# A planned decoder layer: buffers placed by the planner, loads reckoned by run length, v's norm two steps later, and two moves to ScalarE

## The chip, the cores and the metric

The kernel runs on one core of a Trainium2 chip. The time is the device time of one execution in microseconds (us); it was taken three times for the kernel before. Five engines work side by side, each with its own queue of instructions in order: TensorE (PE; its weight loads are shown as PEld), VectorE (DVE), ScalarE (ACT), GpSimd (POOL) and SyncE (SP), which issues most of the transfers between HBM and the on-chip memory. Results of PE land in PSUM, all else lies in SBUF.

## The reference

One layer of a decoder trunk, for a prompt of 1024 tokens and 8 single-token samples, D = 1024, all in float32:

```
xn = rmsnorm(h, pre_g);  u, v, z_a, x_b, z_b, g_a, g_b = split(xn @ w_in)      # 1024 x 7168
vn = layernorm(gelu(v));  s = tril(w_s[g]) @ vn (within chunks of 128 tokens) + b_s[g]
y_a = gelu(u) * s * silu(z_a)
q = trailing mean of x_b over 2/4/8/16 tokens - x_b;  y_b = (q @ w_pool) * scale * silu(z_b)
m = sigmoid(g_a) * (y_a @ w_pa) + sigmoid(g_b) * (y_b @ w_pb)
h = h + rmsnorm(m @ w_out, post_g)
e = p @ w_ple;  h = h + rmsnorm(sigmoid(rmsnorm(h, ple_in_g) @ w_pg) * e, ple_out_g)
```

Further outputs are the normed v of the last chunk and of the samples, and the last rows of x_b.

## The kernel before

**Precision and products.** Every float32 operand is cut into two parts, high and low (`split`, line 341: ACT writes the high part, DVE the rest), and a product is three products on PE (high x high, high x low, low x high; `product`, line 568). The large products are done by a Strassen scheme (`strassen`, line 616): seven products P1 to P7 in place of eight, over quarters of x (B11, B21, B22) and sums of quarters (T1 to T4), and over quarters or sums of the weight. One such product of a quarter is a step: `prepare` cuts its weight part, `run` issues its 12 matmuls of 512 columns (two of 260 where the 8 samples ride along), `evacuate` takes the PSUM result. The first evacuation, of P1, opens a buffer u: ACT copies 512 columns into it and, where the samples ride along, POOL zeroes the last 8 (line 632). Later parts are added to u on DVE.

**Order of the stages.** Opening (`begin`, line 1584): the embedding e = p @ w_ple, the norm and turning of x, the first steps of v. Then v (4 pairs of feature blocks), g_a, u with z_a, x_b with z_b and the pooling, g_b, the products with w_pa and w_pb (all with features on the partitions), and then, with tokens on the partitions (`Tokens`, line 540; PSUM tile `acct`), m @ w_out (`outsteps`) and the gate product with w_pg (`gatesteps`). At the very start PE transposes the identity ten times into a PSUM bank named warm (line 1607).

**v's norm.** v is written to HBM in 32 x 32 blocks (`V.done`, line 870; runs of 128 bytes), read back a chunk of 128 tokens at a time (`v_fetch`), turned back block by block on DVE, summed and squared on ACT (`ln_stats`), scaled (`ln_apply`), cut into vh and vl (`v_split`) and multiplied with the chunk's w_s on PE (`spatial`, PSUM tile `mix`). These calls are hung on the steps of g_a and of the first u and z_a (line 1259): for the n-th chunk at s = 3 + 4n the fetch at step s - 2, the stats and the norm at s, the cut at s + 1, the products at s + 4.

**The gate's norm.** After m @ w_out a tile of h (128 tokens) is scaled by the post norm, h's old value is added by a transfer, its squares are summed on ACT into the buffer hn, DVE scales h into hn (`gate_norm`, line 1382), and PE transposes hn (tile `pht`).

**The planner** (line 55). The program's calls are not issued at once: each is recorded as an Op with an estimated duration. A call of PE advances a clock; `at` of an Op is that clock when it was recorded. `wanted` (line 172) works back from PE's `at` to the latest moment `late` at which each Op must start. `order` (line 195) then plays the engines forward: an Op may start when its inputs are there, its engine is free, and not before min(late - lead, at) + slip; among those that could start, the one with the earliest `late` is taken. So the order on PE may differ from the program's. `slip` is how far PE is behind: start - at of the last PE Op (line 268). A transfer is reckoned at 0.36 MB per us whatever its shape, plus a fixed landing time.

**Slots.** All larger buffers come from a pool of 46 equal slots (line 321). Before, the pool handed out its buffers in turn: `row` in `order` lists freed slots by the order in which their last user was issued, a new buffer takes the front of it, and it waits for that slot's last user. A transfer wants 3 slots to spare.

Of the kernel before, what the change touches and what calls it, by code (L numbers as in the profile page):

```python
# [45 lines left out]

class Taker:
# [7 lines left out]
class Planner:  # L55
# [8 lines left out]
    LOAD, LEAD, PATIENCE, RATE, SPARE = 14.0, 14.0, 60.0, 0.36, 3  # L64
    SPARED = 1.0

    def __init__(self, nc, slots, queues):
        self.nc, self.slots, self.queues = nc, slots, queues
        self.ops, self.seen, self.users, self.tags = [], {}, {}, {}
        self.fixed, self.open, self.clock = True, None, 0.0  # L70
        for e in self.ENGINES:
            setattr(self, e, Taker(self, e))

    def tile(self, ap, tag):

        self.tags[ap.tensor.name] = tag
        return ap

    def space(self, ap):
# [18 lines left out]
        return ap.tensor.name, first, first + parts, tuple(pieces)  # L98

# [38 lines left out]
    def take(self, engine, method, args, kwargs):  # L138
# [56 lines left out]
    def order(self):  # L195
# [10 lines left out]
        row, slip, table, pipe, done = [((0, -1), 0.0)] * self.slots, 0.0, 1, 0.0, 0  # L206
        calls = []
# [4 lines left out]
        def soonest(o):  # L212
# [18 lines left out]
        while done < len(self.ops):  # L231
# [23 lines left out]
            del row[: len(o.fresh)]  # L255
# [11 lines left out]
            elif e == "tensor" and not o.fixed:  # L267
                slip = max(0.0, o.start - o.at)
# [9 lines left out]
            for name in o.names:  # L278
                if name in left:
                    left[name] -= 1  # L280
                    last[name] = max(last[name][0], key), max(last[name][1], end)
                    if not left[name]:
                        row.append((last[name][0], last[name][1] + 0.3))
            row.sort(key=lambda r: r[0])
        return [(e, call) for _, _, e, call in sorted(calls, key=lambda c: c[:2])]

    def play(self, tc):
        with tc.manual_schedule():
            for e, (method, args, kwargs) in self.order():
                getattr(getattr(self.nc, e), method)(*args, **kwargs)  # L290
# [6 lines left out]
def hybrid_step(  # L297
# [9 lines left out]
    spool = ctx.enter_context(tc.tile_pool(name="slots", bufs=SLOTS))  # L307
# [13 lines left out]
    def slot(name, shape=(P, T), dt=F32):  # L321
        n_name[0] += 1
        return plan.tile(spool.tile(list(shape), dt, tag="slot", name=f"{name}_{n_name[0]}", bufs=SLOTS,
                                    padded_shape=None), "slot")
# [39 lines left out]
    for j in range(POOL_BUF):  # L364
        nc.gpsimd.memset(rc[:, j : j + 1], 1.0 / (j + 1))
    nc = plan
# [3 lines left out]

    def rstd(parts, n=P):

        t, r = sm("ms"), sm("rstd")
        nc.vector.tensor_scalar(out=t[:n], in0=parts[0][:n], scalar1=EPS,
                                scalar2=parts[1][:n] if len(parts) == 2 else 0.0, op0=ALU.add, op1=ALU.add)
        nc.gpsimd.tensor_tensor(out=r[:n], in0=t[:n], in1=mhalf[:n], op=ALU.pow)
        return r

    def root(part, n=P):

        t, r = sm("ms"), sm("rstd")
        nc.vector.tensor_scalar(out=t[:n], in0=part[:n], scalar1=EPS, scalar2=None, op0=ALU.add)
# [233 lines left out]
    def strassen(weights, operand, user, form=Features, order=None):  # L616
# [183 lines left out]
    def norm_root(t):  # L800
        xt, n = (xe, NS) if t == S else (xts[t], P)
        roots[t] = root(square_sum(xt[:n], n, scratch=slot("squares", (P, D))), n)
# [6 lines left out]
    nc.scalar.activation(out=warm, in_=mhalf, func=AF.Gelu_apprx_tanh)  # L809
    vecs = slot("vecs", (P, P))  # L810
# [449 lines left out]
    for n, t in enumerate([NB - 1, *range(NB - 1)]):  # L1260
        s = 3 + 4 * n
# [4 lines left out]
        at(flow[s + 4], lambda t=t: spatial(t))  # L1266
# [82 lines left out]
    class Out(User):  # L1349
# [9 lines left out]
        def direct(self, m, j, ps):  # L1359
            t = self.tile(m)  # L1360
            parts[t].append(square_sum(ps))
            nc.scalar.activation(out=h_of[t][:, half(j)], in_=ps, func=AF.Copy)

        def summed(self, m, j, ps, u, free=None):
# [3 lines left out]
            parts[t].append(square_sum(o))  # L1368
# [13 lines left out]
    def gate_norm(t):  # L1382
# [5 lines left out]
        nc.vector.tensor_scalar_mul(hn[:r], h[:r], rs[:r])  # L1388
# [20 lines left out]
    def out_sample():  # L1409
        start(S, "hs")  # L1410
        for j, o in enumerate(sample_product(samples["m"], woop)):
            parts[S].append(square_sum(o[:NS], NS))
# [9 lines left out]
    def gated(t, c, src):  # L1422
# [4 lines left out]
        parts[t].append(square_sum(g, r))  # L1427
        if len(parts[t]) > 2:
            a, b = parts[t][:2]
            both = sm("both")  # L1430
            nc.vector.tensor_scalar(out=both[:r], in0=a[:r], scalar1=b[:r], scalar2=None, op0=ALU.add)
            parts[t][:2] = [both]
# [21 lines left out]
    class Embed(User):  # L1454
        def loads(self):
# [31 lines left out]
    gatesteps = [strassen(Turned(i, "h"), wgop, Embed(i), Tokens, LAST if i == NPAIR - 1 else None)  # L1487
# [15 lines left out]
    at(outsteps[3][4], lambda: gain_row("out", ple_out_g[0]))  # L1503
# [17 lines left out]
    def p_load(h):  # L1521

        praw.append(slot("p", (P, 4, PLE)))
        src = p_prompt[h * HALF : (h + 1) * HALF].rearrange("(p t) c -> p t c", t=4)
        for q in range(2):
            dma(praw[h][:, 2 * q : 2 * q + 2], src[:, 2 * q : 2 * q + 2])
# [57 lines left out]
    def begin():  # L1584
# [22 lines left out]
        for t in range(10):  # L1607
            nc.tensor.transpose(ps[:, t % 4 * P : (t % 4 + 1) * P], ident, ident)
# [6 lines left out]
        embed_out(0, 0)  # L1615
# [87 lines left out]
```

## Time and profile before

| | |
|---|---|
| median of 3 runs | 1004.33 us (1003.48 to 1004.35) |
| the profiled execution, its own time | 1005.86 us |
| its span, first to last instruction | 1004.2 us |
| mean granted clock of PE | 0.993 |
| moved by DMA | 169.04 MB, 168 GB/s over the span |

The busy times in a row of a view are sums over an engine's instructions. The windows of the trace cut the span into stretches and give each engine's busy time in it, then PE's granted clock as a share of full speed, the share of time that the 16 DMA engines were busy, and the GB/s they moved. The waits give, for each engine and tile, the instruction that it waited for: total, times, longest. A row of the timeline gives the start, the duration, the engine and the operation (written tile <- read tiles), and in square brackets how long the engine had been idle before it and what ended that.

### The profile page before, as it was taken

Reading aid. Unit: us, or ns where it says so; the run is one execution under the profiler, and the core shown is the slowest. Engines: PE = TensorE matmul, PEld = TensorE weight load, DVE = VectorE, ACT = ScalarE, POOL = GpSimd, SP = SyncE. Lnnn points to the kernel's source line nnn. Section 1 sums busy time; section 2 is a strip of 40 time slices with the busy share of each in tenths; the row PEclk is TensorE's granted clock in tenths of the full one; section 3 lists DMA queues with packets and bytes.
Section 4 is the critical chain, followed back from the end, with each engine's and each line's share of the span. In section 5 each row is a group of like instructions: output and inputs, shape, how many; then the busy total and the mean of one; then the engine's idle time right before and its main releaser. Section 6 shows DMA issues by size and latency. Waiting matters only on the chain. (4 is left out here: it accounts for less than half of the span.)

```text
span 1004.2 us, 16017 instructions
## 1 busy us (share of the span) xinstructions
PE 984.5 (98%) x6122; PEld 883.1 (88%) x6122; DVE 805.0 (80%) x1239; ACT 487.5 (49%) x845; POOL 81.8 (8%) x162
## 2 busy tenths in 40 slices
PE   8999999999999999999999999999999999998996
PEld 6899988999999999999999999999999988887885
DVE  5698458887788898887776987697799898779796
ACT  7764345666434334232433333552353365678563
POOL 1230000000000000000010100000000002312121
PEclk9999999899999999999999999999999999999998
DMA  9364644333365676441304075973754543397437
GB/s 352 130 148 85 148 105 170 105 127 106 126 221 199 231 273 202 166 170 53 123 15 156 28 257 208 314 279 125 246 218 150 181 153 84 87 304 262 128 78 218
DMA packets 120033, 169.04 MB, mean 168 GB/s; under 512 B 40830, under 2 KB 79790, under 8 KB 119949
## 3 DMA queue, kind: packets, MB, share of 16 engines
q1 hardware_dynamic: 117589, 160.11, 47.0%
q0 software_dynamic: 2048, 7.37, 4.3%
q8 instruction: 48, 0.79, 0.3%
q10 hardware_dynamic: 320, 0.54, 0.2%
q14 instruction: 28, 0.23, 0.1%
HBM read 116.69 MB, written 51.77 MB: 168 GB/s over the span
## 5 line engine op out<-in xcount | busy, mean ns | idle before, releaser
L290 DVE TENSOR_TENSOR u<-acc,u 128x520 f32<-128x520 f32 (+1 forms) x90 | 62.4, 694 | 35.1 <-PE acc L290 31.7
L290 POOL TENSOR_TENSOR rstd<-ms,mhalf 128x1 f32<-128x1 f32 (+1 forms) x45 | 41.0, 913 | 229.7 <-DVE ms L290 214.6
L290 POOL MEMSET u<- 128x8 f32 x35 | 3.6, 104 | 553.4 <-PE acc L290 302.5
L290 ACT ACTIVATE u<-acc 128x512 f32<-128x512 f32 x39 | 23.2, 594 | 37.0 <-PE acc L290 36.4
L290 ACT ACTIVATE paw<-pas 128x512 fp32r<-128x512 f32 x16 | 10.0, 628 | 31.2 <-DVE pas L290 25.9
L290 DVE TENSOR_TENSOR big<-big 128x1024 f32<-128x1024 f32 (+4 forms) x20 | 24.5, 1263 | 0.0
L290 DVE TENSOR_TENSOR xb<-acc,u 128x520 f32<-128x520 f32 (+1 forms) x12 | 8.3, 693 | 19.1 <-PE acc L290 19.1
L290 ACT ACTIVATE zbw<-zbs 128x512 fp32r<-128x512 f32 x16 | 9.9, 628 | 27.8 <-DVE zbs L290 24.5
L290 ACT ACTIVATE pbw<-pbs 128x512 fp32r<-128x512 f32 x16 | 10.0, 629 | 27.2 <-DVE pbs L290 24.0
L290 ACT ACTIVATE big<-pht,gvec 128x128 f32<-128x128 f32 x64 | 17.9, 396 | 7.0 <-PE pht L290 7.0
L290 PE MATMUL accm<-qh,wpoolw 128*128 128x260 f32 (+1 forms) x96 | 20.9, 319 | 0.0
L290 ACT ACTIVATE big<-mix 128x256 f32<-128x256 f32 x32 | 12.0, 381 | 16.9 <-PE mix L290 16.1
L290 DVE TENSOR_TENSOR acc<-acc,u 128x512 f32<-128x512 f32 (+1 forms) x16 | 11.2, 697 | 8.7 <-PE acc L290 8.7
L290 PE MATMUL mix<-wst,vh 128*128 128x256 f32 x64 | 16.6, 335 | 1.4 <-ACT vh L290 0.8
L290 ACT ACTIVATE gbw<-gbs 128x512 fp32r<-128x512 f32 x16 | 10.0, 626 | 15.1 <-DVE gbs L290 12.6
L290 DVE SCALAR_TENSOR_TENSOR zb<-accm,gvec,zb 128x512 f32<-128x512 f32 (+1 forms) x16 | 12.0, 751 | 6.5 <-PE accm L290 6.4
L290 PEld LDWEIGHTS accm<-qh,wpoolw 128*128 128x128 f32 x96 | 15.6, 188 | 1.9
L290 ACT ACTIVATE xbw<-xbs 128x512 fp32r<-128x512 f32 x16 | 9.8, 625 | 15.0 <-DVE xbs L290 12.8
L290 ACT ACTIVATE gb<-gb 128x1032 f32<-128x1032 f32 (+1 forms) x8 | 6.8, 854 | 18.2 <-DVE gb L290 18.2
L290 PE MATMUL mix<-wst,vl 128*128 128x128 f32 x64 | 14.7, 230 | 0.9 <-DVE vl L290 0.9
L290 ACT ACTIVATE uw<-us 128x512 fp32r<-128x512 f32 x16 | 9.9, 626 | 11.5 <-DVE us L290 6.2
L290 DVE TENSOR_TENSOR gaw<-gas,gaw 128x512 fp32r<-128x512 f32 x16 | 11.0, 686 | 5.7 <-ACT gaw L290 5.6
(691 smaller groups left out, 3614.0 us busy)
## 6 DMA issues: line engine op xcount, KB each, us to landing
ga<-ga SPq DMA_DIRECT2D x16, 516.0 KB
gb<-gb SPq DMA_DIRECT2D x16, 516.0 KB
ya<-za SPq DMA_DIRECT2D x8, 516.0 KB
yb<-zb SPq DMA_DIRECT2D x8, 516.0 KB
x<-in_x_prompt_dram SPq DMA_DIRECT2D x8, 512.0 KB
vraw<-in_w_in_dram SPq DMA_DIRECT2D x8, 512.0 KB
e<-e SPq DMA_DIRECT2D x8, 512.0 KB
vturned<-v SPq DMA_DIRECT2D x32, 128.0 KB
```

Source lines behind the costliest of these rows:

```text
L290: getattr(getattr(self.nc, e), method)(*args, **kwargs)
```

## The change

- Loads: a transfer's size is weighed by its shortest contiguous run (`run`): (1 + 0.2 / run in KB), at a rate of 0.42 in place of 0.36 MB per us; one that accumulates counts twice and lands after 3.5 in place of 4.5.
- Slots: each slot has its own buffer. The planner picks the slot when it places an Op: of those already free at that moment in its reckoning, the one freed last (for Ops of the fixed opening the one freed first). An Op waits for as many free slots as it needs. Buffers are made when the plan is played (`View`, `slot`, `real`).
- slip is PE's start less the work that PE has done, not less the Op's own place in the program.
- v's norm: s = 5 + 4n, and the products at s + 5.
- ACT zeroes the end of u (from a constant), after its copy; ACT scales h into hn.
- The opening: nine matmuls of 512 columns with a zeroed tile `heat` (DVE sets it) in place of ten transposes; the first cut of e on DVE; w_ple's first half in two transfers; three short vector loads from ACT's queue to SP's, and w_ple's second half ahead of them.
- Sums of squares of a tile are added as they come (`gather`); the loads for the gate's tiles (`ge_start`) and the gain row for the output are hung on steps later than before (the gain row on the gate's second step in place of the fifth of the last product with w_out).

The core of the diff:

```
@@ Planner @@
-    LOAD, LEAD, PATIENCE, RATE, SPARE = 14.0, 14.0, 60.0, 0.36, 3
+    LOAD, LEAD, PATIENCE, RATE, SPARE = 14.0, 14.0, 60.0, 0.42, 3
...
+    def run(ap):
+        n = 1
+        for s, m in reversed(list(ap.ap)[0 if "DRAM" in str(ap.space) else 1 :]):
+            if m == 1:
+                continue
+            if s != n:
+                break
+            n *= m
+        return min(n * 4e-3, 4.0)
...
-            op.busy, op.moved = 1.0 if engine == "gpsimd" else 0.45, writes[0].size() * 4e-6
-            op.lands = 4.5 if kwargs.get("accum_op") is not None else 2.0
+            run = min(self.run(a) for a in (writes[0], reads[0]))
+            op.busy, op.moved = 1.0 if engine == "gpsimd" else 0.45, writes[0].size() * 4e-6 * (1 + 0.2 / run)
+            op.lands = 2.0
+            if kwargs.get("accum_op") is not None:
+                op.moved, op.lands = 2 * op.moved, 3.5
...
-                t = max(t, *(end for _, end in row[: len(o.fresh)]), *(key[1] for key, _ in row[:need] if key[0]))
+                t = max(t, row[len(o.fresh) - 1][0])
...
-            del row[: len(o.fresh)]
+            could = [r for r in row if r[0] <= now + 1e-9]
+            for name in sorted(o.fresh):
+                r = could.pop(0 if o.fixed else -1)
+                row.remove(r)
+                self.place[name] = r[1]
...
-                slip = max(0.0, o.start - o.at)
+                slip = max(0.0, o.start - worked)
+                worked += o.busy
...
-                        row.append((last[name][0], last[name][1] + 0.3))
-            row.sort(key=lambda r: r[0])
+                        row.append((max(last[name][1] + 0.3, key[1] if key[0] else 0.0), self.place[name]))
+            row.sort()
@@ hybrid_step @@
+    none = cpool.tile([P, NS], F32, tag="none", name="none")
+    nc.gpsimd.memset(none, 0.0)
...
+    def gather(parts, part, n=P):
+        if parts:
+            so_far = sm("sofar")
+            nc.vector.tensor_scalar(out=so_far[:n], in0=parts[-1][:n],
+                                    scalar1=EPS if len(parts) == 1 else parts[0][:n], scalar2=None, op0=ALU.add)
+            parts[:] = [so_far]
+        parts.append(part)
...
+                nc.scalar.activation(out=at["u"][:, :HALF], in_=ps, func=AF.Copy)
                 if form.tail:
-                    nc.gpsimd.memset(at["u"][:, HALF:], 0.0)
-                nc.scalar.activation(out=at["u"][:, :HALF], in_=ps, func=AF.Copy)
+                    nc.scalar.activation(out=at["u"][:, HALF:], in_=none, func=AF.Copy)
...
+    heat = slot("heat", (P, HALF), F32R)
+    nc.vector.memset(f32(heat), 0.0)
...
-        s = 3 + 4 * n
+        s = 5 + 4 * n
...
-        at(flow[s + 4], lambda t=t: spatial(t))
+        at(flow[s + 5], lambda t=t: spatial(t))
...
-        nc.vector.tensor_scalar_mul(hn[:r], h[:r], rs[:r])
+        nc.scalar.activation(out=hn[:r], in_=h[:r], func=AF.Copy, scale=rs[:r])
...
-    at(outsteps[3][4], lambda: gain_row("out", ple_out_g[0]))
+    at(gatesteps[0][1], lambda: gain_row("out", ple_out_g[0]))
+    for i, e in enumerate(embeds):
+        at(gatesteps[i - 1][4] if i else outsteps[3][6], e.begin)
...
-        we.fetch(0, nc.scalar)
+        raw = we.raw[0, 0] = slot("weraw", (P, 2, HALF))
+        for k in range(2):
+            dma(raw[:, k], w_ple[k * P : (k + 1) * P, :HALF], nc.scalar)
         for t in range(4):
             x_load(t)
+        we.fetch(1)
         for i, v in enumerate((pre_g, pool_scale, ple_in_g)):
-            dma(vecs[i * NB : (i + 1) * NB, :], v[0].rearrange("(k p) -> k p", p=P), nc.scalar)
-        we.fetch(1)
+            dma(vecs[i * NB : (i + 1) * NB, :], v[0].rearrange("(k p) -> k p", p=P))
...
-        for t in range(10):
-            nc.tensor.transpose(ps[:, t % 4 * P : (t % 4 + 1) * P], ident, ident)
+        for t in range(9):
+            plan.apart()
+            nc.tensor.matmul(ps, heat[:, :P], heat, start=True, stop=True)
...
-        embed_out(0, 0)
+        embed_out(0, 0, True)
```

More of the change, by code (lines that the diff above doesn't have):

```diff
@@ L205, in order @@
         rings["scalar"] = rings["sync"]
-        row, slip, table, pipe, done = [((0, -1), 0.0)] * self.slots, 0.0, 1, 0.0, 0
-        calls = []
+        row, slip, table, pipe, done = [(0.0, i) for i in range(self.slots)], 0.0, 1, 0.0, 0
+        calls, worked = [], 0.0
         for o in self.ops:
@@ L369, in hybrid_step @@
     big = cpool.tile([P, NB, T], F32, tag="big", name="big")
+    def gather(parts, part, n=P):
[5 more added lines that the diff above has]
+        parts.append(part)
     def rstd(parts, n=P):
         t, r = sm("ms"), sm("rstd")
[L374 to L382, printed above, removed]
+        nc.vector.tensor_scalar(out=t[:n], in0=parts[-1][:n], scalar1=EPS if len(parts) == 1 else parts[0][:n],
+                                scalar2=None, op0=ALU.add)
         nc.gpsimd.tensor_tensor(out=r[:n], in0=t[:n], in1=mhalf[:n], op=ALU.pow)
@@ L801, in norm_root @@
         xt, n = (xe, NS) if t == S else (xts[t], P)
-        roots[t] = root(square_sum(xt[:n], n, scratch=slot("squares", (P, D))), n)
+        roots[t] = rstd([square_sum(xt[:n], n, scratch=slot("squares", (P, D)))], n)
     def norm_scale(t):
@@ L1426, in gated @@
         mul(g, e_of[t][:r, c], g)
[L1427 to L1432, printed above, removed]
+        gather(parts[t], square_sum(g, r), r)
         if t >= NB - 2:
@@ L1454, in hybrid_step, with begin @@
     class Embed(User):
-        def loads(self):
+        def begin(self):
             for m in range(2):
```

61 lines of the change are left out of this document (51 added, 10 removed).

## The prediction

> **What bounds the kernel now.** I read the busy times on the page first, then the windows of 25 us, the waits of PE, short windows where PE stood idle, and the timeline around those places.
>
> ```profile
> PE 984.5 (98%) x6122; PEld 883.1 (88%) x6122; DVE 805.0 (80%) x1239; ACT 487.5 (49%) x845; POOL 81.8 (8%) x162
> ```
> ```profile
> 0.00:25.00 25.00, 21.13 (x100) 17.11 (x100) 12.65 (x24) 17.76 (x29) 4.34 (x27) 1.00 0.99 353
> ...
> 125.00:150.00 25.00, 23.23 (x148) 20.36 (x147) 12.29 (x23) 11.56 (x20) 1.47 (x5) 1.00 0.46 106
> 150.00:175.00 25.00, 23.27 (x164) 21.20 (x162) 22.13 (x40) 13.42 (x23) 1.91 (x3) 1.00 0.48 170
> 175.00:200.00 25.00, 24.51 (x148) 22.97 (x149) 21.05 (x40) 15.45 (x28) 1.54 (x2) 0.87 0.32 106
> ...
> 500.00:525.00 25.00, 25.00 (x167) 22.92 (x166) 18.54 (x29) 6.05 (x11) 3.35 (x6) 1.00 0.11 34
> ...
> 900.00:925.00 25.00, 22.19 (x104) 17.52 (x103) 23.08 (x31) 22.43 (x46) 5.72 (x6) 1.00 0.94 322
> ...
> 975.00:1000.00 25.00, 20.20 (x100) 16.79 (x98) 20.69 (x37) 11.03 (x27) 5.74 (x7) 0.95 0.85 224
> ```
> The columns are the stretch, its length, the busy time of PE, PEld, DVE, ACT and POOL, the granted clock, the DMA share and GB/s. PE is the bound: 984.5 of 1004.2 us. A middle window such as 500 to 525 us is full, so no work taken from another engine gains there; it can only lose. The 19.7 us of idle PE lie in few places: 25 - 21.13 = 3.87 us in the opening, 1.77 + 1.73 + 0.49 = 3.99 us between 125 and 200 (where v is normalised), 2.81 us between 900 and 925 (the start of the gate product), and the rest, some 9 us, is the end after the last matmul. One loss is not idle time: the clock is 0.87 between 175 and 200. So what the change can gain is the opening, v's norm with its clock, and the gate's start.
>
> ```profile
> PE acct L290 <- DVE ms L290: 1.6, 1, 1.6
> PE acc L290 <- DVE ms L290: 1.5, 1, 1.5
> PE acct L290 <- DVE hw L290: 1.2, 1, 1.2
> PE mix L290 <- DVE vl L290: 0.9, 1, 0.9
> PE mix L290 <- ACT vh L290: 0.8, 1, 0.8
> PE mix L290 <- DVE big L290: 0.5, 1, 0.5
> ```
> Each of these is one event, so the schedule that the planner writes is nearly right everywhere and wrong at about five points.
>
> **v's norm, two steps later.** The planner's moved calls (v_fetch, ln_stats, ln_apply, v_split) start at flow[5 + 4n] instead of flow[3 + 4n]; the mix products of the chunk come at +5 instead of +4, so three steps later in all. What failed before:
>
> ```profile
> 147.81 1.21 DVE L290 TENSOR_TENSOR sv<-sv,lng 8x1024 f32<-8x1024 f32 x1
> 148.95 0.68 DVE L290 TENSOR_TENSOR ga<-acc,u 128x520 f32<-128x520 f32 x1
> 149.68 0.51 PE L290 MATMUL acc<-xB22h,gaw 128*128 128x260 f32 x2 [1.48 <-DVE ms L290]
> 165.75 1.25 DVE L290 STREAM_TRANSPOSE big<-vblocks 128x1024 f32<-128x1024 f32 x1 [1.74 <-DMA vblocks<-vturned]
> 172.69 0.39 PE L290 MATMUL mix<-wst,vh 128*128 128x256 f32 x1 [0.83 <-ACT vh L290]
> 173.95 0.33 PE L290 MATMUL mix<-wst,vl 128*128 128x128 f32 x1 [0.87 <-DVE vl L290]
> ```
> At 149.68 PE waits 1.48 us; the evacuation that frees its PSUM region (ga, 148.95 to 149.63) stood behind a 1.21 us norm step in DVE's strict queue. At 172.69 and 173.95 it waits for vh and vl; DVE had itself stood 1.74 us for the block from HBM. After that the clock falls:
>
> ```profile
> 174.50:176.00 1.50, 0.98 (x8) 0.83 (x6) 1.50 (x6) 0.83 (x3) 0.00 (x0) 0.63 0.00 0
> 176.00:178.00 2.00, 2.00 (x11) 2.00 (x10) 1.97 (x6) 1.96 (x5) 0.00 (x0) 0.50 0.00 0
> 178.00:180.00 2.00, 2.00 (x11) 2.00 (x11) 2.00 (x5) 2.00 (x4) 0.55 (x1) 0.50 0.00 0
> 180.00:182.00 2.00, 2.00 (x12) 2.00 (x12) 1.14 (x2) 1.44 (x2) 0.00 (x0) 0.57 0.63 262
> ```
> The clock's loss is length times (1 - clock): 1.5 x 0.37 + 2 x 0.5 + 2 x 0.5 + 2 x 0.43 = 3.4 us. With the waits of 1.48, 0.83, 0.87 and 0.52 this place costs 7.1 us, nearly half of it by the clock. Each chunk moves its fetch on SP, its transpose, norm and cut on DVE, two sums and a cut on ACT and a root on POOL, past the weight loads and cuts of two steps; nothing is added to them. A step is 12 products of 512 columns, 2.8 us (12 x 0.23, the spacing in the opening below). Between fetch and mix there is now one step more, 2.8 us, above the 2.2 us that vh, vl and the next mix were late, and the first fetch comes two steps (5.6 us) after it did, when v's last turned blocks are out. The new reckoning of loads helps the same place: v's turned writes go in runs of 128 bytes, which the planner now counts 1 + 0.2/0.128 = 2.6 times as long as before per byte. What is late next is DVE, at 21 to 22 us of 25 from 150 to 200, with SP behind it (a store of a normed tile waits in SP's queue for DVE, and block fetches behind the store); the moved work is carried into 200 to 260. I take 6.0 us of the 7.1 as gained; bounds 7.1 and 0.
>
> **The opening.** Ten transposes of the identity become nine products of a zeroed 128x512 tile; the first cut of e goes to DVE; w_ple comes in two pieces; the three vector loads go from ACT's queue to SP's.
>
> ```profile
> 1.93 2.40 PE L290 MATMUL warm<-ident 128*128 128x128 f32 x10 [1.93 <-POOL ident masks.py:199]
> 6.84 0.60 ACT L290 ACTIVATE ph<-pp 128x512 fp32r<-128x512 f32 x1 [4.54 <-DMA p<-in_p_prompt_dram]
> 8.60 0.63 PE L290 MATMUL e<-wehi,pl 128*128 128x512 f32 x1
> 9.03 0.63 PE L290 MATMUL e<-wehi,ph 128*128 128x512 f32 x1
> 11.58 0.39 PE L290 MATMUL e<-wehi,pl 128*128 128x512 f32 x1
> 11.80 0.39 PE L290 MATMUL e<-wehi,ph 128*128 128x512 f32 x1
> 12.92 1.03 ACT L290 ACTIVATE e<-e 128x1024 f32<-128x1024 f32 x1 [1.89 <-PE e L290]
> 25.96 0.48 PE L290 MATMUL acc<-xB11h,vw 128*128 128x512 f32 x1
> ```
> ```profile
> 8.01:11.34 3.33, 3.33 (x8) 2.67 (x9) 2.53 (x6) 3.02 (x6) 0.55 (x1) 1.00 1.02 411
> ```
> The products of e start 0.43 us apart (8.60, 9.03) until 11, then 0.23 (11.58, 11.80), although the clock column of the window says 1.00: the spacing shows a cold array that the column doesn't. Eight products in 3.33 us would take 8 x 0.23 = 1.8 warm, so 1.5 us are lost. Nine zero products take 9 x 0.43 = 3.9 us; with a memset of DVE ahead, behind which all of PE's queue stands (no row; between nothing and the 0.7 us of a 128x512 step of DVE), they run from about 1.5 to 5.5 us. p's transposes of the first half then wait till 5.5 us, covered: their cut stood until 6.84 us on ACT anyway. That cut can now begin at about 6.1 us, since ACT no longer issues vector loads; worth 0.7 us if w_ple has landed. Against it stands DMA: its share is 0.99 over the first 25 us, and x and w_in still come at the same rate, so part of what PE gains it waits out later. The vector loads lengthen SP's queue ahead of w_in's first tiles, which nobody needs before 25.96 us. Moving e's 1.03 us from ACT to DVE (about 1.4 us there, two pieces of 0.7) relieves ACT, busy 17.76 us of 25 against DVE's 12.65. Bounds: 0 (all is given back to DMA) and 2.2 (1.5 + 0.7). I take 1.3, a little over the middle, since the rows show both an array that is cold and DMA engines that are full.
>
> The Trainium skill's page "TensorE: Matmul & The Clock Gate", Part 4, says that transposes do not count as busy for the gate; the trace agrees (PE transposed from 1.93 us on and was still cold at 9.03). But Part 1 of that page speaks against the change: one idle window of about 3.4 us brings the gate down again, and between the zero products and e there are only transposes. By it the opening could keep its cold products; this is the second rival.
>
> **The gate's start.** The scaling of h goes to ACT, 8 tiles and the sample.
>
> ```profile
> L290 ACT ACTIVATE hn<-h x8: 1042/1060/1078, 845.6 to 923.1; 128x1024 f32<-128x1024 f32 x8
> L290 DVE TENSOR_SCALAR hn<-h,rstd x8: 731/746/753, 849.5 to 927.7; 128x1024 f32<-128x1024 f32 x8
> 914.59 2.35 DVE L290 TENSOR_TENSOR wgT4l<-wgT,wgT4h 128x1024 fp32r<-128x1024 f32 x2
> 916.86 0.68 DVE L290 TENSOR_TENSOR hw<-big,hw 128x512 fp32r<-128x512 f32 x1
> 917.60 0.73 PE L290 MATMUL acct<-wgT4h,hw 128*128 128x512 f32 x2 [1.24 <-DVE hw L290]
> ```
> PE waits at 917.60 for a cut that DVE did after two cuts of wg, with no gap: DVE is full. Two of the moved steps fall into 900 to 925: DVE loses 1.5 us of 23.08, ACT gains 2.1 us on 22.43, 24.5 of 25. So the bound may only change hands. And it is ACT's queue that now stands while POOL works out a tile's root, with wg's cuts behind it. The later loads (e's tiles and the gain row come three to four steps later) free slots for wg, and better slots let cuts start early. Bounds: 2.8 us gained (all idle gone) and 2 us lost (ACT's 2.1 us laid on the path). I take 0.8 gained.
>
> **What costs nothing.** The 8 columns at the end of u go from POOL to ACT:
>
> ```profile
> L290 POOL MEMSET u<- 128x8 f32 x35 | 3.6, 104 | 553.4 <-PE acc L290 302.5
> ```
> ACT has no such row; between POOL's 0.10 us and the 0.60 us of a 128x512 step (ph above) that is 3.6 to 21 us, nearer the low end for 8 columns, on an ACT that is idle half the time; that idleness is the cover, and the gate's stage has no such end. The sums of squares add some DVE steps of 0.15 to 0.2 us, one a tile, off PE's path; in the end phase only a sum that was already off the chain moves. So the 9 us at the end stay.
>
> **The slots.** Before, a load took the buffer that came round; now the planner names it, and loads take the one freed last in its reckoning.
>
> ```profile
> SPq L290 <- PE acc L290: 180.9, 46, 23.3
> ```
> SP already stands 180.9 us, 46 times, for PE to let go of a buffer, and PE loses nothing by it in the middle: there is much cover. If the real run is behind the reckoning, the buffer freed last is the one still in use, and one load that stands holds every load behind it on SP. The new rate, 0.42, with the charge for short runs is about 0.40 for runs of 4 KB; the trace shows 411 GB/s from 8 to 11 us but 353 over the first 25, so it is the fast end. The skill's page "DMA: Bandwidth & Descriptors", Specifications, gives about 358 GB/s of HBM a core, by which the reckoning would be too fast; here the 411 stands against that as a limit, the 353 for it as a mean. I charge 0.6 us for new small stalls; bounds 0 and one event like that at 172.69 (2.2 + 3.4 = 5.6 us).
>
> **Sum.** -6.0 - 1.3 - 0.8 + 0.6 = -7.5 us. The profiled execution took 1005.86 us (its span 1004.2), 1.5 above the median of 1004.33; the difference is taken from both: 998.4 for such an execution, 996.8 for the median.
>
> **Rivals.**
> 1. The norm still stalls. DVE at 21 of 25 us is as full as before and PE's queue is strict, so the wait only comes three steps later and the clock falls once more: the 6.0 becomes 0.5, and the time 1002.3. For it: the 1.48 us wait was one of queue order. Against: 2.8 us more slack than the 2.2 us missing. Chance 0.20.
> 2. The change doesn't do what it says: the zero products do not leave the array warm, or DMA takes it back. Opening 0, time 998.1. Chance 0.13.
> 3. Slower: the buffer freed last makes SP's head stand in the full middle, and a cut comes late. Each event costs up to 5.6 us; the change has 8.1 us to lose, so from two such events on it is slower: 1004.33 - 8.1 + 2 x 5.6 = 1007.4. For it: the 46 waits; against: they cost nothing so far. Chance 0.14.
>
> **How the numbers follow.** The forecast has 0.53; its own range is 992 to 1001. About 0.2% (2 us) is what a measurement of this kernel can tell from no change. Faster by more: the forecast, rival 2, and half of rival 1 (its 1002.3 is on the border): 0.53 + 0.13 + 0.10 = 0.76. Same: the other half of rival 1 and a little of rival 3 (one event and some): 0.12. Slower: 0.12. The low end is all bounds together, 1004.33 - 7.1 - 2.2 - 2.8 = 992.2, and 1.1 us for what is left of the opening's 3.87: 991.1. The high end takes in rival 1 and stops short of rival 3: 1004.
>
> **What would show it.** Right: no PE wait over 1 us and a clock of 1.00 between 125 and 260 us; e's products 0.23 us apart from the first; the first product of x's first quarter with w (25.96 us before) at 24.7 or so; a wait or two under 1 us for hw or wg between 900 and 925, now on ACT. Wrong: a window between 200 and 900 where PE is under 24.5 us, with SP waiting for PE just ahead of it (rival 3); a clock of 0.5 after a mix (rival 1); 0.43 us between e's products (rival 2).

## The result, and the profile after

The changed kernel took 997.76 us (median of 4 runs, 997.43 to 998.06), the kernel before 1003.97 us beside it (1003.48 to 1004.35): a ratio of 0.9938, 95% interval 0.9921 to 0.9956, 6.2 us faster. The forecast was 996.8 us. In a second set of runs, on another chip, the changed kernel took 999.27 us and the kernel before 1002.63 us, ratio 0.9967 (0.9953 to 0.9982). The sign is the same, the size about half; the opening of the experiments below says what is known of the reason.

The busy times on the page of the changed kernel:

```profile
span 996.1 us, 15937 instructions
...
PE 982.0 (99%) x6121; PEld 879.7 (88%) x6121; DVE 804.0 (81%) x1250; ACT 504.6 (51%) x888; POOL 77.8 (8%) x128
```

The windows of 25 us up to 975 us in which PE was not full, and the two at the norm in which it was (stretch, length, busy time of PE, PEld, DVE, ACT, POOL, then clock, DMA share, GB/s):

```profile
0.00:25.00 25.00, 23.24 (x113) 18.79 (x113) 16.26 (x28) 19.74 (x31) 5.25 (x28) 1.00 0.99 347
...
125.00:150.00 25.00, 24.46 (x167) 21.89 (x165) 14.94 (x27) 11.22 (x19) 1.21 (x2) 1.00 0.56 127
150.00:175.00 25.00, 25.00 (x174) 23.25 (x174) 21.95 (x42) 15.55 (x30) 1.50 (x2) 1.00 0.43 150
175.00:200.00 25.00, 25.00 (x178) 23.46 (x178) 22.66 (x44) 18.91 (x36) 2.33 (x3) 1.00 0.44 148
...
300.00:325.00 25.00, 24.61 (x161) 22.15 (x160) 23.83 (x36) 11.24 (x19) 0.00 (x0) 1.00 0.53 188
...
800.00:825.00 25.00, 24.51 (x128) 20.43 (x127) 24.01 (x32) 14.19 (x20) 0.95 (x1) 1.00 0.36 134
...
900.00:925.00 25.00, 23.01 (x108) 18.14 (x107) 23.96 (x34) 23.14 (x48) 5.79 (x6) 1.00 0.82 266
```

And the waits of PE:

```profile
PE acct L353 <- DVE ms L353: 1.6, 1, 1.6
PE warm L353 <- DVE heat L353: 1.5, 1, 1.5
PE acct L353 <- DVE gb L353: 0.5, 1, 0.5
PE acc L353 <- DVE ga L353: 0.4, 1, 0.4
PE acct L353 <- DVE hw L353: 0.4, 1, 0.4
PE acc L353 <- DVE u L353: 0.4, 1, 0.4
PE e L353 <- DVE pl L353: 0.2, 1, 0.2
```

The reader is to see that every wait at the norm is gone but one of 0.4 us, with a clock of 1.00 in every window up to 975 us, that two small waits have come up in windows that were full before (0.39 us at 300 to 325, 0.49 us at 800 to 825), and that the gate's start still waits. In the order of the prediction, between the two profiled executions:

| place | before | after | gained | forecast |
|---|---|---|---|---|
| v's norm, waits of PE (125 to 200 us) | 3.99 | 0.54 | 3.45 | 6.0, both |
| v's norm, the clock's loss | 3.4 | 0 | 3.4 | |
| first product of x with w, cleared of p's transposes | 25.56 | 23.51 | 2.05 | 1.3 |
| gate's start, waits (900 to 925 us) | 2.81 | 1.99 | 0.82 | 0.8 |
| new waits in the full middle | 0 | 0.88 | -0.88 | -0.6 |

(p's second transposes, 0.4 us, stood ahead of that product before and stand behind it now.) The sum is 8.8 us; the last product of PE moved from 994.92 to 986.90, 8.0 us, so 0.8 us is not placed. The medians differ by 6.2, since the profiled execution of before was 1.9 us above its median. That execution (1005.86 us) is also slower than each of the 92 of the same kernel that were timed later (999.15 to 1005.69), so the table shows the gain over a slow execution, not over a usual one.

The opening in the timeline of the changed kernel:

```profile
0.99 0.48 DVE L353 MEMSET heat<- 128x512 f32 x1 [0.99 <-PEq L1770]
1.53 4.21 PE L353 MATMUL warm<-heat 128*128 128x512 f32 x9 [1.53 <-DVE heat L353]
5.53 1.86 PE L353 MATMUL pp<-ident,p 128*128 128x128 f32 x8
8.33 0.39 PE L353 MATMUL e<-wehi,ph 128*128 128x512 f32 x1
8.56 0.39 PE L353 MATMUL e<-wehi,pl 128*128 128x512 f32 x1
23.51 0.50 PE L353 MATMUL acc<-xB11h,vw 128*128 128x512 f32 x1
```

The zero products run from 1.53 to 5.74 us. e's first three products start 0.73 and 0.33 us apart (the second waits 0.23 us for pl), and from the third on they are 0.23 us apart (8.33, 8.56) instead of 0.43. Between them PE only transposed, 5.53 to 7.27 us, and did not get cold: the second rival did not come about. The Trainium skill, "TensorE: Matmul & The Clock Gate", Part 1, gives about 3.4 us of idleness before the gate falls; 1.7 us of transposes are within that, and here the trace agrees.

### The profile page after: what moved, and what is told of

Same layout as the page of the kernel before. It is cut to its first block, busy times and chain, and to the rows that moved or that the text cites. A ratio compares the mean times of both kernels' runs of the same rounds, so it can differ in the third digit from the quotient of the medians.

```text
span 996.1 us, 15937 instructions
## 1 busy us (share of the span) xinstructions
PE 982.0 (99%) x6121; PEld 879.7 (88%) x6121; DVE 804.0 (81%) x1250; ACT 504.6 (51%) x888; POOL 77.8 (8%) x128
## 5 line engine op out<-in xcount | busy, mean ns | idle before, releaser
L353 POOL TENSOR_TENSOR rstd<-ms,mhalf 128x1 f32<-128x1 f32 (+1 forms) x45 | 37.6, 838 | 230.3 <-DVE ms L353 223.9
L353 POOL COPY big<-xb 128x1 f32<-128x1 f32 x8 | 3.2, 405 | 262.7 <-ACT xb L353 221.7
L353 DVE TENSOR_TENSOR zbw<-zbs,zbw 128x512 fp32r<-128x512 f32 x16 | 11.0, 690 | 12.3 <-ACT zbw L353 12.2
L353 ACT ACTIVATE xbw<-xbraw 128x512 fp32r<-128x512 f32 x12 | 7.5, 625 | 17.8 <-DMA xbraw<-in_w_in_dram 11.2
L353 ACT ACTIVATE zaw<-zas 128x512 fp32r<-128x512 f32 x16 | 10.0, 628 | 12.2 <-DVE zas L353 8.3
L353 DVE TENSOR_TENSOR paw<-pas,paw 128x512 fp32r<-128x512 f32 x16 | 10.9, 687 | 6.0 <-ACT paw L353 5.9
L353 ACT ACTIVATE gbw<-gbraw 128x512 fp32r<-128x512 f32 x12 | 7.5, 626 | 15.9 <-PE acc L353 7.9
```

The source lines that it names most:

```text
L353: getattr(getattr(self.nc, e), method)(*(self.real(a) for a in args), **{k: self.real(a) for k, a in kwargs.items()})
```

## The experiments

Each set ran on one chip, with the kernel before on the same chip; a ratio is to that. Chips and executions differ, and one difference was seen in all sets, the mean clock of an execution. Of the 14 profiled executions of this case, the 4 with a mean clock of 0.997 keep 1.00 from 125 to 200 us, and the 10 with a lower mean lose some of it there. Of 92 executions of the kernel before, 36 had a mean of 0.997 or more and a median of 1000.5 us, 23 had 0.995 or 0.996 and 1002.4 us, and 33 had 0.994 or less and 1003.5 us. The instructions are the same. So something like the 3.4 us that the prediction took from its one profiled execution are lost in about a third of the executions there, and less or nothing in the others. That the others lose it at the norm too is inferred from their means, since only one execution of the kernel before was profiled. The changed kernel had 0.997 or more in 13 of 16. The four times of the kernel before beside the first result (1003.5 to 1004.4 us) are like those of a fallen clock.

The waits are not the only thing that brings it down. In the profiles of nine of the twelve experiments (all but 5, 7 and 8) the clock falls to 0.5 between 148 and 155 us, 1 to 4 us after sixteen products of 8 columns for the samples (tile smix) begin. In experiments 2, 3, 9 and 12 PE had not waited between 125 us and the fall. Experiment 9, whose norm is that of the changed kernel, and then the changed kernel at the same product:

```profile
148.08 1.95 PE L353 MATMUL smix<-diag,sv 8*128 8x8 f32 x16
...
152.00 0.64 PE L353 MATMUL acc<-xT2l,gaw 128*128 128x260 f32 x2
```
```profile
151.59 0.40 PE L353 MATMUL acc<-xT2l,gaw 128*128 128x260 f32 x2
```
```profile
150.00:175.00 25.00, 25.00 (x161) 23.22 (x161) 21.23 (x39) 13.51 (x25) 2.00 (x2) 0.93 0.38 129
```

PE is full in the window of experiment 9 (the last row), yet from 152 us two products of 260 columns take 0.64 us, where the changed kernel's, behind the same sixteen products (149.37 us), take 0.40. The other way round, two waits of 0.87 and 0.52 us at 171 and 173 us in experiment 3 brought no fall. The same page of the Trainium skill, Part 1, says that the gate looks at a free-running window, by which the same stretch could lie in it otherwise from one execution to the next; no run shows the window. The one idle window of about 3.4 us that this part of the Trainium skill asks for is not borne out at the norm: the fall in experiment 9 came without a wait, behind 1.95 us of small products.

**1. The planner alone.** v's norm, the opening, the scaling of h and the end of u go back to before; what stays is the reckoning, the slots, slip, the late loads and the gathered sums.

```
-        s = 5 + 4 * n
+        s = 3 + 4 * n
...
-        nc.scalar.activation(out=hn[:r], in_=h[:r], func=AF.Copy, scale=rs[:r])
+        nc.vector.tensor_scalar_mul(hn[:r], h[:r], rs[:r])
...
```

> The changed planner (load reckoning, slots, slip) with the late loads of the gate's tiles and the gathered sums; v's norm, the opening, the scaling of h and the end of u as before. Theory (the time comes from v's later norm and the warm opening, the planner itself gives nothing): about 1003.5 us, PE waits for vh or vl near 172 us with a clock of 0.5 after it, products of e 0.43 us apart. Rival (the better reckoning of the turned writes and the named slots cure the norm's wait by themselves): 998 to 999 us, clock of 1.00 from 150 to 200 us.

Measured: 1008.78 us (before 1000.83), ratio 1.0075 (1.0050 to 1.0101). Both theories missed: it is slower. Waits of PE and two windows of this kernel:

```profile
PE smix L353 <- DVE nmean L353: 2.3, 1, 2.3
PE acct L353 <- DVE ms L353: 2.2, 1, 2.2
...
PE pht L353 <- DVE hn L353: 1.8, 1, 1.8
...
PE acc L353 <- DVE xB21l L353: 0.9, 1, 0.9
```
```profile
900.00:925.00 25.00, 22.00 (x100) 16.76 (x98) 20.83 (x28) 21.11 (x43) 6.76 (x5) 1.00 0.98 326
925.00:950.00 25.00, 23.23 (x102) 19.09 (x103) 22.01 (x39) 17.36 (x45) 5.85 (x6) 0.93 0.34 88
```

The norm's wait is not cured, it has another form: PE waits 2.3 us for the samples' norm (smix), and with the clock 4.0 us are lost from 125 to 200 us, against 7.2 before. At the gate's start PE now loses 3.0 + 1.8 us and 1.75 us of clock (25 x 0.07) against 2.8 before, with one wait for hn, which DVE scales here. The rest of the 8 us is not placed: the two profiled executions are only 3.8 us apart, and up to 975 us the windows lose 15.8 us of waits and clock here and 13.9 before.

**2. v's norm alone**, on the kernel before.

```
-        s = 3 + 4 * n
+        s = 5 + 4 * n
...
-        at(flow[s + 4], lambda t=t: spatial(t))
+        at(flow[s + 5], lambda t=t: spatial(t))
```

> The kernel before with only v's norm two steps later and its products three. Theory: 4 to 6 us faster than before (998 to 1000 us), no clock below 1.00 from 125 to 260 us, a wait of PE under 1 us there. Rival (the planner's reckoning does it): 1003 to 1004 us, the wait only moved by two steps.

Measured: 1009.43 us (before 1000.83), ratio 1.0080 (1.0060 to 1.0100). Slower again. At its own place it does gain: PE's waits from 125 to 200 us are 0.88 us in place of 3.99, and the clock there loses 25 x 0.07 = 1.75 us in place of 25 x 0.13 = 3.25; that fall comes at 151 us, ahead of the one wait at 172. But 270 us later, where the kernel before was full, stands this (PE, then SP, then the window):

```profile
442.14 0.80 PE L290 MATMUL accm<-qh,wpoolw 128*128 128x512 f32 x1 [3.95 <-ACT wpoolw L290]
```
```profile
417.40 0.63 SPq L290 DMA_DIRECT2D yalow<-ya  x1
428.79 0.34 SPq L290 DMA_DIRECT2D yalow<-za  x1
...
438.50 0.41 SPq L290 DMA_DIRECT2D wpool<-in_w_pool_dram  x1
```
```profile
425.00:450.00 25.00, 20.74 (x117) 18.14 (x116) 20.00 (x32) 9.19 (x14) 0.00 (x0) 0.86 0.41 138
```

SP issues nothing from 418 to 428.8 us: a store at its head (yalow from za) waits 10.7 us for DVE. The kernel before stood 10.4 us at this place too, and issued the load of w_pool at 433.8. New is a second stand of 4.3 us, up to 433.5, at the next store, again for DVE; the load of w_pool stands behind it and is issued at 438.5. PE loses 4.3 us and the clock 25 x 0.14 = 3.5 us more. Against the profiled execution of before these places account for the whole difference: the span is 3.4 us longer, and the waits and the clock up to 975 us cost 17.3 us against 13.9. It is the form of the prediction's third rival, a load behind a head of SP that stands, but the head waits for a result of DVE and not for a buffer, and no named slot is in this kernel: an order that comes out a little otherwise is enough.

**3. The opening alone**, on the kernel before.

```
+    heat = slot("heat", (P, HALF), F32R)
+    nc.vector.memset(f32(heat), 0.0)
...
-            nc.tensor.transpose(ps[:, t % 4 * P : (t % 4 + 1) * P], ident, ident)
+            plan.apart()
+            nc.tensor.matmul(ps, heat[:, :P], heat, start=True, stop=True)
...
```

> The kernel before with only the new opening (zero products, e's first cut on DVE, w_ple in two pieces, vector loads on SP). Theory: 2 us faster than before (1002 us), first product of x's first quarter with w 2 us earlier than 25.96 us. Rival (the zero products gain only together with the other changes, or DMA takes it back): 1004 us.

Measured: 1001.79 us (before 1000.83), ratio 0.9996 (0.9985 to 1.0007): no gain in the median. In its profile the first product of x with w starts at 24.78 us, 1.2 us earlier than at 25.96. But the clock: none of its 12 executions had 0.996 or more, against 18 of 23 of the kernel before in the same set. In its profile the clock falls at 152 us, 2.5 us after smix begins, with no wait of PE since 125 us, and loses 25 x 0.07 = 1.75 us, more than the 1.2 us that the opening gained. Why it falls in each of these executions, and in few of the kernel before, is not shown.

**4. All but v's norm.** The changed kernel with the norm at its old steps (the edit of experiment 2 turned round).

> The changed kernel with v's norm at its old steps. Theory: 4 to 6 us slower than the changed kernel (1002 to 1004 us), the wait and the fallen clock back near 172 us. Rival (the planner's reckoning does it): 998 us, clock 1.00 there.

Measured: 1002.73 us (before 1000.83), ratio 1.0013 (1.0000 to 1.0026), against 0.9938 and 0.9967 for the changed kernel. As expected in size. Waits of PE, a window, and a step of DVE ahead of the waits:

```profile
PE smix L353 <- DVE sv L353: 2.0, 1, 2.0
...
PE rowsum L353 <- DVE big L353: 0.6, 1, 0.6
```
```profile
150.00:175.00 25.00, 24.43 (x158) 22.98 (x157) 20.22 (x39) 13.86 (x26) 0.56 (x1) 0.90 0.43 148
```
```profile
142.42 1.25 DVE L353 STREAM_TRANSPOSE big<-vblocks 128x1024 f32<-128x1024 f32 x1 [2.03 <-DMA vblocks<-vturned]
```

At the old steps DVE stands 2.0 us for the first block, as in the prediction, and the samples' norm behind it on DVE comes 2.0 us late for PE. Behind that the clock falls, at 148 us, and costs 1.0 us up to 150 and 2.5 us (25 x 0.10) after it; 9 of the 12 executions had a mean clock of 0.994 or less, none of the 12 of the changed kernel in experiment 5. In this planner the later steps are worth about 0.46 to 0.75% (4.6 to 7.5 us; 1.0013 against 0.9967 and 0.9938, on other chips).

**5. The changed kernel again**, on another chip.

> The changed kernel once more, beside the kernel before on the same chip. The kernel before now took 1000.8 us in most executions and 1003 to 1005 us in those with a mean clock of 0.992 to 0.994. Theory (the gain is 3 to 4 us of waits, and 3.4 us more whenever the clock falls at v's norm before): 997 to 998 us, about 3 us under the kernel before if that keeps its clock, 6 if not. Rival (the two chips differ as a whole): the ratio of 0.994 returns whatever the clock of before is.

Measured: 999.27 us (before 1002.63), ratio 0.9967. The rival is out: the 0.994 did not return. The kernel before had 6 of 29 executions with a mean clock of 0.997 or more, the changed kernel 9 of 12. The time expected was 1 to 2 us too low and the gain too large: the 6 executions of before that kept their clock have a median of 1000.5 us, 1.3 us above the changed kernel and not 3. The profiled execution (998.20 us) has new waits for hn (1.0 us) and u (0.8 us); why others took up to 1002.4 us is not known.

**6. DVE scales h.**

```
-        nc.scalar.activation(out=hn[:r], in_=h[:r], func=AF.Copy, scale=rs[:r])
+        nc.vector.tensor_scalar_mul(hn[:r], h[:r], rs[:r])
```

> The changed kernel with DVE scaling h, as before. Theory (DVE is the full engine at the gate's start, and transposes of hn wait for it): 2 to 4 us slower than the changed kernel, PE waiting 3 us or more between 900 and 930. Rival (ACT is as full, the wait only changes hands): within 1 us of the changed kernel.

Measured: 1002.49 us (the changed kernel 999.27 in the same set), ratio to before 0.9995 (0.9981 to 1.0010). Its waits of PE and its window at the gate's start:

```profile
PE acct L353 <- DVE ms L353: 2.2, 1, 2.2
PE pht L353 <- DVE hn L353: 1.7, 1, 1.7
```
```profile
900.00:925.00 25.00, 20.40 (x89) 15.38 (x88) 22.96 (x34) 20.46 (x39) 8.29 (x7) 1.00 0.93 304
```

PE loses 4.6 us in that window instead of 2.3 in the changed kernel beside it (22.73 busy), which however waits 1.0 us for ACT's hn in the window ahead: 1.3 us more from 875 to 925 us. The median is 3.2 us longer, but not by the gate's start alone: the clock is 0.93 from 150 to 175 us here (1.75 us) and 1.00 in the changed kernel's two profiles, and none of the 12 executions had a mean of 0.997, against 9 of 12. So the move gains at its place, 1.3 to 2.6 us (4.60 against 3.29 and 1.99 in the two profiles), although ACT takes longer for a tile than DVE did (1.14 us for 0.75).

**7. Transposes first.**

```
-        for t in range(9):
-            plan.apart()
-            nc.tensor.matmul(ps, heat[:, :P], heat, start=True, stop=True)
+        for t in range(10):
+            nc.tensor.transpose(ps[:, t % 4 * P : (t % 4 + 1) * P], ident, ident)
...
```

> The changed kernel with the ten transposes in place of the nine zero products; the rest of the new opening stays. Theory (zero products warm the array, transposes don't): e's products 0.43 us apart for some 3 us, the whole 1 to 2 us slower than the changed kernel. Rival (the transfers set the opening): cold products but the same time within 0.5 us.

Measured: 1000.10 us (the changed kernel 999.27), ratio to before 0.9974 (0.9960 to 0.9987); the interval overlaps that of the changed kernel. In its timeline:

```profile
9.14 0.63 PE L353 MATMUL e<-wehi,pl 128*128 128x512 f32 x1
9.56 0.63 PE L353 MATMUL e<-wehi,ph 128*128 128x512 f32 x1
...
25.11 0.50 PE L353 MATMUL acc<-xB11h,vw 128*128 128x512 f32 x1
```

e's products are cold again (0.43 us apart), and the first product of x with w comes 1.6 us later than at 23.49 in the run beside it. At its place the effect is clear; in the whole time 0.8 us, which the runs do not part from nothing.

**8. The slot freed first.**

```
-                r = could.pop(0 if o.fixed else -1)
+                r = could.pop(0)
```

> The changed kernel, but every Op takes the slot freed first among those free. Theory of the prediction's third rival (the slot freed last makes SP stand): 0 to 1 us faster, the waits of 0.4 us at 146, 323 and 811 us gone, SP waiting less for PE. Other theory (which free slot is taken matters little beside the order it leads to): SP's waits about as long, the time within 2 us either way.

Measured: 997.74 us (6 runs; the changed kernel 999.27), ratio to before 0.9951 (0.9933 to 0.9969). The waits of 0.4 us at 146, 323 and 811 us are gone in its profile, one of 0.3 us has come at 550 to 575. SP's waits for PE did not shrink, as the theory had it, but grew: 195.8 us and 50 times, against 132.3 and 33, and PE lost nothing by them. It is the fastest version run, but its interval overlaps that of the changed kernel: that taking the slot freed last costs something is likely, not shown.

**9. The gate's cuts a step earlier.**

```
-    turn_over(wgop, l, [*l[2:], c[0], c[1]])
+    turn_over(wgop, l, [*l[1:], c[0]])
```

> The changed kernel with the cuts of the gate's weight one step (2.8 us) earlier. Theory (the wait of 2.0 us between 900 and 925 is DVE's and ACT's crowding by these cuts; the 25 us ahead have room, DVE 20 and ACT 22 of 25): PE's waits there fall under 1 us, 1 to 2 us faster than the changed kernel. Rival (the free slots, not the engines, hold the cuts back): no change within 0.5 us, or new waits for slots ahead.

Measured: 998.98 us, ratio to before 0.9970 (0.9955 to 0.9984), the same as the changed kernel. The cuts did not move. The last cut of wg and the step ge of DVE, for which PE waits, in the changed kernel, then here:

```profile
912.93 2.35 DVE L353 TENSOR_TENSOR wgB22l<-wgB,wgB22h 128x1024 fp32r<-128x1024 f32 x2
...
915.80 0.69 DVE L353 TENSOR_TENSOR ge<-acct,u 128x512 f32<-128x512 f32 x1
```
```profile
911.94 2.34 DVE L353 TENSOR_TENSOR wgB22l<-wgB,wgB22h 128x1024 fp32r<-128x1024 f32 x2
...
914.81 0.67 DVE L353 TENSOR_TENSOR ge<-acct,u 128x512 f32<-128x512 f32 x1
```

All is 1.0 us earlier, as the whole execution is, and in the same order: where the program hangs a cut did not bind it, which leaves the planner's times. So the test says nothing of the crowding itself; PE's wait of 1.56 us ends in both with ge, which stands on DVE behind two cuts of 1.2 us.

**10. The old reckoning of loads.**

```
-    LOAD, LEAD, PATIENCE, RATE, SPARE = 14.0, 14.0, 60.0, 0.42, 3
+    LOAD, LEAD, PATIENCE, RATE, SPARE = 14.0, 14.0, 60.0, 0.36, 3
...
-            op.busy, op.moved = 1.0 if engine == "gpsimd" else 0.45, writes[0].size() * 4e-6 * (1 + 0.2 / run)
-            op.lands = 2.0
-            if kwargs.get("accum_op") is not None:
-                op.moved, op.lands = 2 * op.moved, 3.5
+            op.busy, op.moved = 1.0 if engine == "gpsimd" else 0.45, writes[0].size() * 4e-6
+            op.lands = 4.5 if kwargs.get("accum_op") is not None else 2.0
```

> The changed kernel with the old reckoning of loads (0.36 for every run length, accumulating loads 4.5 to land and counted once). Theory (the two steps cure the norm, the reckoning adds little): within 2 us of the changed kernel, PE waiting under 1 us between 125 and 200. Rival (the reckoning of the short runs is what keeps the fetched blocks from coming late): a wait of 1 to 2 us at the norm and a fallen clock, 3 to 6 us slower.

Measured: 1006.55 us (before 1001.84), ratio 1.0052 (1.0034 to 1.0069), some 8 us above the changed kernel. The rival was right. DVE, then PE:

```profile
141.18 0.69 DVE L351 TENSOR_TENSOR gas<-garaw,garaw 128x512 f32<-128x512 f32 x1 [3.81 <-DMA garaw<-in_w_in_dram]
```
```profile
149.22 0.51 PE L351 MATMUL acc<-xB22h,gaw 128*128 128x260 f32 x2 [2.23 <-DVE ga L351]
```

DVE stands 3.8 us for a weight load that is queued behind v's turned writes (it is in the changed kernel too, where DVE stands 1.8 us), the samples' norm slides behind it, and the evacuation ga behind that; in that window PE loses 3.25 us. In the next the clock is 0.93, but so it is in experiments 6, 9 and 11, which have the new reckoning. So in the new planner the later steps alone do not keep the norm free of waits; the reckoning is needed too. The profiled execution is the fastest of the six, and the trace does not place the 3.1 us from it to the median.

**11. POOL zeroes the end of u.**

```
-                nc.scalar.activation(out=at["u"][:, :HALF], in_=ps, func=AF.Copy)
                 if form.tail:
-                    nc.scalar.activation(out=at["u"][:, HALF:], in_=none, func=AF.Copy)
+                    nc.gpsimd.memset(at["u"][:, HALF:], 0.0)
+                nc.scalar.activation(out=at["u"][:, :HALF], in_=ps, func=AF.Copy)
```

> The changed kernel with POOL zeroing the end of u again, ahead of ACT's copy. Theory (35 small steps on an ACT that is half idle cost nothing): within 1 us of the changed kernel. Rival (POOL's step ahead of the copy holds up the evacuation where POOL is busy with a root): 1 to 2 us slower, waits for u.

Measured: 999.80 us, ratio to before 0.9982 (0.9969 to 0.9995) against 0.9967 (0.9953 to 0.9982) for the changed kernel: unclear. No wait for u came up in its profile.

**12. The old slip.**

```
-                slip = max(0.0, o.start - worked)
+                slip = max(0.0, o.start - o.at)
```

> The changed kernel with slip as before (start less the Op's own place). Theory (with PE's steps out of program order the old slip is too large and holds cuts and loads back): 2 to 5 us slower than the changed kernel, with waits of PE for cuts. Rival (of the planner's three edits the reckoning of loads alone matters): within 1.5 us of the changed kernel, ratio to before 0.995 to 0.998.

Measured: 1005.28 us (before 1002.33), ratio 1.0033 (1.0020 to 1.0047): 6 us or so above the changed kernel. Two of its windows:

```profile
350.00:375.00 25.00, 23.27 (x147) 20.38 (x145) 23.04 (x36) 8.04 (x13) 0.00 (x0) 1.00 0.89 322
...
900.00:925.00 25.00, 21.40 (x95) 16.51 (x93) 21.22 (x31) 21.79 (x43) 6.50 (x7) 1.00 0.96 318
```

Waits have spread over the full middle (1.7 us in the first, for u and the cuts of za) and over the gate's start (3.6 us), besides a clock of 0.96 and 0.97 at the norm, behind smix.

## Why the prediction was right, and where not

The time, the sign and the places were right; the clock at the norm and the planner were not. That the time came within 1 us is in part luck: the first set met the kernel before at 1003.5 to 1004.4 us, and the second gives 999.27 us and a gain of 3.4.

**v's norm.** Right at its place, between the two profiles: waits 3.99 to 0.54 us, clock back to 1.00. Mis-sized was the clock's term: 3.4 us was taken from one execution as if each lost it. In the 92 executions of before a third had a mean of 0.994 or less, 3.0 us above those with 0.997 or more, and a quarter lay between, 1.9 us above them. Its cause was taken too simply as well: "After that the clock falls" puts it down to the waits, but in experiments 2, 3, 9 and 12 it falls behind smix with none, so a norm without waits does not by itself keep the clock. The credit, "Between fetch and mix there is now one step more", holds on the kernel before: the steps alone leave 0.88 us of waits (experiment 2). In the new planner the reckoning is more than the help that the prediction made it: the reckoning without the steps leaves 2.5 us of waits and 3.5 us of clock (experiment 4), the steps without the reckoning 3.25 us of waits (experiment 10).

**The opening.** 2.05 us at its place against 1.3, and 1.2 by itself (experiment 3); the zero products have their share in it (1.6 us in experiment 7), and PE is full from 25 to 50 us, so the transfers did not take it back there. At its place the middle value was too careful; in the whole time neither experiment 3 nor 7 parts the gain from nothing.

**The gate's start.** 0.8 us forecast and found, all of it in the wait for hw (1.24 us before, 0.43 after). The larger wait, which stood in the prediction's list and was not followed up there, did not move:

```profile
924.64 0.47 PE L290 MATMUL acct<-wgB22h,hw 128*128 128x512 f32 x1 [1.57 <-DVE ms L290]
```
```profile
916.63 0.47 PE L353 MATMUL acct<-wgB22h,hw 128*128 128x512 f32 x1 [1.56 <-DVE ms L353]
```

That "the bound may only change hands" came true in part: in the second profile of the changed kernel PE waits 1.0 us for ACT's hn. But with DVE scaling h more is lost there, 4.60 us against 3.29 and 1.99 (experiment 6). The price of the step was judged by the sums of busy time, DVE 23 and ACT 22 of 25; what decided was which queue stands between PE and its next step, and that was mostly DVE's.

**What costs nothing.** The end of u: 35 steps of 0.193 us on ACT, 6.8 us, in the range given and near its low end; no wait of PE ends with them in either form. Hidden, as said. (In the low end of the range, 3.87 - 2.2 leaves 1.7 of the opening, not 1.1; the forecast does not hang on it.)

```profile
L353 ACT ACTIVATE u<-none x35: 188/193/211, 64.9 to 780.5; 128x8 f32<-128x8 f32 x35
```
```profile
L353 ACT ACTIVATE hn<-h,rstd x8: 1136/1140/1157, 841.7 to 919.8; 128x1024 f32<-128x1024 f32 x8
```

**The planner.** This step failed: it was charged 0.6 us and otherwise taken as neutral. New waits of 0.88 us fit the 0.6, but by itself the planner's part makes the kernel 8 us slower (experiment 1), and inside the changed kernel its reckoning is worth some 8 us and its slip some 6, by the medians (experiments 10 and 12). And the sum of the parts failed with it: forecast gains of 6.0 for the norm and 1.3 for the opening became a loss of 8.6 us and nothing (ratio 0.9996) when each was done alone. The planner writes one order out of all its inputs, so that a part moved at 140 us puts a load behind a standing head of SP at 440 us. A load behind a standing head of SP, as in the third rival, was seen only there, in a variant and with a head that waits for DVE; in the changed kernel SP waited less for PE than before (132.3 us and 33 times, before 180.9 and 46).

What stays open: why the clock falls behind smix in one execution and not in another, where the planner alone loses all its 8 us, whether the slot freed last costs the 1.5 us that experiment 8 suggests, and why the sum of the places is 0.8 us above the move of PE's end.

## What to carry to other kernels

With a planner that orders everything, read the gain of a change at its place in the trace and the cost of it over the whole span; a part tried alone says little of its worth in company, here not even the sign. A price read from one execution may be one that many executions do not pay: look at the clock of each run before counting a fallen clock as a fixed cost. A fall of the clock need not stand behind a wait: look at the small products ahead of it too. Where two engines are equally busy, it can pay to move work off the one whose queue stands ahead of the bound, even if the other takes half as long again.

## What the runs showed of the hardware that was not expected

Zeroed operands warm the array: nine products of zeros, 4.2 us, and e's products soon run 0.23 us apart, where ten transposes leave them at 0.43. Sixteen products of 8 columns, 1.95 us in which the trace calls PE busy, were followed within 4 us by a clock of 0.5 in 9 of the 14 profiled executions, in experiment 9 without any wait near it. The same instructions lose a clock in one execution and not in another: 0.991 to 0.998 as the mean clock of the kernel before, 999.2 to 1005.7 us. ACT needs 1.14 us to copy 128x1024 with a scale for each partition, DVE 0.75 us, and a step of 8 columns still takes ACT 0.19 us.
